# Order of the first loads, of the sines and of the input norms in the opening stage of a GLA / Hyena diffusion step

## The chip, the cores and the metric

One core of a Trainium2 chip runs the kernel. The metric is device microseconds, the median of several executions; lower is better. The core has TensorE (PE, with its weight loads PEld), VectorE (DVE), ScalarE (ACT), GpSimd (POOL) and SyncE (SP); the last three also issue DMAs, each from its own queue.

## The reference, cut to what matters

The whole model step has two layers (one with GLA and retention heads, one with Hyena convolutions and an RG-LRU). The change touches what comes ahead of the first layer's projections:

```python
mod = silu(cond) @ w_mod[layer] + b_mod[layer]              # (1024) @ (1024, 3072), two layers
shift, scale, gate = split(mod, 3)
h = rms_norm(x, norm_g[layer]) * (1 + scale) + shift        # x: 1024 + 128 tokens of 1024

def hyena_filters(L, ...):                                  # L = 1024 and 128
    g = sin(freq1 * (feats @ w1 + b1))
    g = sin(freq2 * (g @ w2 + b2))
    filt = (g @ w3 + b3).reshape(L, 4, 1024)
    return filt * exp(-t * deltas)[:, None, :]
# the Fourier transform of filt is what the long convolutions of layer 2 read
```

## The kernel before

The program is written with a tile framework whose scheduler sets the order on each engine when the kernel is built; each engine then works through its own list strictly in that order and waits on semaphores. `issue_after(x)` and `high_priority(n)` move work in that order.

**The opening stage** (`phase0`) does four things and then `phase1` begins with its projections (`pp` on TensorE).

- The filter network (`filter_mlp`): `ft` times `w1`, a range reduction on VectorE (`fold`, tiles `sv` and `sk`), a sine on ScalarE (tile `g1`), times `w2`, again `fold` and sine (`g2`), for 1152 positions in four pieces of 288. The result goes as a high and a low part into `GA` and `GB`.
- Eight filters (`filters`, n = 0 to 7). Of each, 40 tap products (`mm<-wa,GA` and `mm<-wb,GB`, 256 columns) are multiplied on VectorE by the window `win`, an exponential made on ScalarE (tile `fa`). VectorE's butterflies make an even half (`fd`) and an odd half (in `fa`) from it. TensorE then takes nine leaf groups of four products each (`mm<-fd,fw` and `mm<-fa,fw`): the five even ones, the tap products of filter n+1, the four odd ones. ScalarE copies each group out (`fH`), SyncE stores it to `h_dram`.
- The modulation (`modulation`): for each of two layers, 64 products of the conditioning (`cond`, 32 columns) with 384 columns of `w_mod` into four column groups of PSUM tile `mod`. The 64 loads of `w_mod` (384 KB each, two products) go through GpSimd's queue, from the start on. Two products are issued at a time, as one step of a generator that the leaf groups advance. Layer 0 is done in two parts: three quarters (24 loads) with the first filter, the rest at the end.
- The inputs: x has nine tiles of 128 tokens. A first pass (`start`, beside filter 1) loads all nine on ScalarE's queue into two buffers and takes their sums of squares; `rstd` then gives all nine scales at once. A second pass (`h_tiles`, three tiles after each of filters 1, 2 and 7) loads x again (`x0`), scales it on ScalarE, transposes it on TensorE (`tr<-ident,x`, eight per tile), applies the modulation on ScalarE (`htmp`), and splits it into `hh` (ScalarE) and `hl` (VectorE), which the projections read.

ScalarE uses two activation tables: one with the natural logarithm and the exponential, one with the sine. In the order before, six of the first 18 windows stand ahead of the first sine, and 12 behind the last.

Of the kernel before, what the change touches and what calls it, by code (L numbers as in the profile page):

```python
# [17 lines left out]
P = 128  # L18
# [150 lines left out]
class Step:  # L169
# [61 lines left out]
    def rstd(self, pool, ms, shape, tag, scale=1.0):  # L231

        v = self.t(pool, shape, tag + "v")
        r = self.t(pool, shape, tag + "r")
        q = self.t(pool, shape, tag + "q")
# [10 lines left out]
    def setup(self, po):  # L246
        i, pc = self.i, self.pc
        self.ident = pc.tile([P, P], F32, name="ident")
        self.ld(self.ident, i["k_ident"])
# [4 lines left out]
        self.rows = [po.tile([P, 2, CH], F32, name=f"rows{k}") for k in range(2)]  # L254
# [49 lines left out]
    def modulation(self, layer, p, psm, js=(0, 8), more=None):  # L304
# [3 lines left out]
        row = self.rows[layer]  # L308
        bias = self.t(p, [P, 2, CH], "htmp")
        parts = [(b, max(js[0] - 4 * b, 0), min(js[1] - 4 * b, 4)) for b in range(2)]  # L310
        parts = [x for x in parts if x[1] < x[2]]
        self.nc.gpsimd.memset(bias, 0.0)
        for b, lo, hi in parts:
            for g in range(lo, hi):
                for r in range(2):
                    at = (4 * b + g) * CH
                    self.ld(bias[32 * g + r:32 * g + r + 1, b], i["b_mod"][layer:layer + 1, at:at + CH])
        n = 2
        todo = [(k, j) for k in range(KT) for j in range(*js, n)]
        ws = []  # L320

        def load():
            k, j = todo[len(ws)]
            w = self.t(more, [P, n * CH], "wm", bufs=4) if more and len(ws) % 7 < 4 else self.t(self.pr, [P, D], "wr")[:, :n * CH]
# [11 lines left out]
        for b, lo, hi in parts:  # L336
            s = slice(32 * lo, 32 * hi)
            self.tt(row[s, b], acc[s, b, :CH], bias[s, b], OP.add)
            if b:
                self.sto(self.row_dram[layer, s], row[s, b])  # L340
        if js[0]:
            return
# [30 lines left out]
    def norm_tile(self, p, x, junk, out, tag="n"):  # L373
# [4 lines left out]
        self.ts(out, x, r, OP.mult)  # L378
# [39 lines left out]
    def mlp_loads(self, pt):  # L418
# [4 lines left out]
        ft = self.t(pt, [33, n], "ft")  # L423
        for q, name in enumerate(("hy_b1", "hy_freq1", "hy_b2", "hy_freq2")):
# [9 lines left out]
    def filter_mlp(self, p, pt, ps, loads):  # L434
# [6 lines left out]
        hv, w1, ft, w2 = loads  # L441
        GA = self.t(p, [P, 2 * n + P], "GA", F32R)
# [16 lines left out]
        for c in range(2):  # L459
# [5 lines left out]
            self.ts(v, pm[:, :m], hc[:, 1:2], OP.mult, hc[:, 0:1], OP.add)  # L465
            self.fold(pt, v, g1[:, s], "sk")
        for e in range(2):
            h = slice(64 * e, 64 * e + 64)
            for c in range(2):
# [3 lines left out]
                self.ts(v, pm[:, :m], hc[:, 3:4], OP.mult, hc[:, 2:3], OP.add)  # L473
# [15 lines left out]
        self.nc.gpsimd.dma_start(GB[64:], i["k_ones"])  # L489
# [70 lines left out]
    def windows(self, pt, g):  # L560
# [7 lines left out]
        self.window(0, 18 if g else 6)  # L568
# [34 lines left out]
    def filters(self, p, pi, pt, G, ps, w, others, first, rest):  # L603
# [19 lines left out]
        def leaves(n, g, o, ks, E, L, prompt):  # L623
            for k in ks:
                if n != 1:
                    with self.tc.issue_after(self.last_mm.ins):
                        for z in range(1 if n else 2):
                            next(rest if n else first, None)
                pm = self.t(ps, [P, 512], "mm")
                if k < 8:  # L630
                    self.leaf(pm[:, :C], pm[:, C:], (L, E), k)
                else:
                    for e in range(2):
# [4 lines left out]
                evac = self.nc.scalar.copy(H[:, :, :2].rearrange("p b r c -> p r b c"),  # L638
                                           pm.rearrange("p (r b c) -> p r b c", r=2, b=2))
# [5 lines left out]
            return evac  # L645
# [1055 lines left out]
```

## Time and profile before

| What | us |
|---|---|
| median of 3 executions | 2502.75 (2501.25 to 2506.71) |
| profiled execution, device time | 2499.16 |
| its span | 2497.2 |
| opening stage, to the first `pp` product | 308 |
| TensorE busy in the span | 2414.1 (97%) |

The profile gives the busy time of each engine, the granted clock of TensorE, the DMA traffic, the chain of work that ended last, and for each instruction what ended the idle time ahead of it (in square brackets). TensorE's records overlap, so starts rather than lengths give the pace. A 32-bit product of the leaves or of the modulation leaves two records.

### The profile page before, as it was taken

The page shows a single profiled execution, that of the slowest core. Times are in us where ns is not written, and L with a number is a line of the kernel's source. Part 1 is how long each engine was busy: PE and PEld are TensorE (multiplying, and loading weights), DVE is VectorE, ACT ScalarE, POOL GpSimd, SP SyncE. Part 2 cuts the span into 40 slices and gives each one's busy share as a digit, 9 for nine tenths or more (in the row PEclk, how much of TensorE's full clock was granted, in tenths as well). Part 3 has the DMA queues.
Part 4 walks back from the last instruction along what each step waited for, and adds up shares of the span by engine and source line. Part 5 has one row for each costly group of instructions (what it writes and reads, how often), then busy time and mean ns, then how long its engine had stood idle before and what let it go on. Part 6 is the DMA issues. An engine that isn't in the chain of part 4 may idle for free.

```text
span 2497.2 us, 38502 instructions
## 1 busy us (share of the span) xinstructions
PE 2414.1 (97%) x14681; PEld 2201.0 (88%) x14681; DVE 1660.5 (66%) x3970; ACT 1071.1 (43%) x2355; POOL 72.7 (3%) x149
## 2 busy tenths in 40 slices
PE   5799799999999999999999999999999999999998
PEld 2666699999999999997888999999999999998786
DVE  6588657686664464564234688878887897888632
ACT  4555556564543343353224332223222328888311
POOL 2011000000000000000000000000000000000000
PEclk9899899999999999999999999999999999999999
DMA  7677511121211212225334421222122212114431
GB/s 226 199 233 208 183 47 46 54 60 31 56 52 51 61 46 54 60 83 179 106 115 149 146 65 60 63 72 69 57 62 75 65 43 62 62 62 142 154 98 41
DMA packets 201080, 230.68 MB, mean 92 GB/s; under 512 B 13823, under 2 KB 171743, under 8 KB 200448
## 3 DMA queue, kind: packets, MB, share of 16 engines
q1 hardware_dynamic: 188120, 175.01, 23.1%
q0 software_dynamic: 11104, 48.27, 6.0%
q10 hardware_dynamic: 1672, 4.95, 0.7%
q8 instruction: 115, 1.88, 0.3%
q14 instruction: 69, 0.57, 0.1%
HBM read 172.27 MB, written 55.91 MB: 91 GB/s over the span
## 4 chain that ended last, share of the span: by engine, by line
PE 85%; DVE 6%; ACT 4%; DMA 3%; issue 2%; SPq 0%; POOL 0%; DVEq 0%; ACTq 0%; POOLq 0%
PE pp L211 45%; PE po L211 14%; PE mm L211 5%; PE X L211 5%; PE pd L211 5%; PE o L211 3%; PE tr L215 2%; PE kv L211 2%; PE pg L211 2%; PE mod L211 1%; PE sc L211 1%; PE kv L215 1%; DVE fa L200 1%; DMA wr<-h_dram 1%; DVE cs L200 1%
## 5 line engine op out<-in xcount | busy, mean ns | idle before, releaser
L211 PE MATMUL pp<-gh,wl 128*128 128x384 f32 x1152 | 392.6, 341 | 0.0
L211 PE MATMUL pp<-gh,wh 128*128 128x384 f32 x1152 | 391.6, 340 | 0.7 <-ACT raw L1293 0.6
L211 PE MATMUL pp<-gl,wh 128*128 128x384 f32 x1152 | 391.1, 340 | 0.4 <-DVE gl L200 0.4
L211 PE MATMUL pp<-wh,hh 128*128 128x256 f32 x1152 | 332.7, 289 | 0.0
L211 PE MATMUL pp<-wh,hl 128*128 128x256 f32 x1152 | 328.7, 285 | 0.0
L211 PE MATMUL pp<-wl,hh 128*128 128x256 f32 x1152 | 326.2, 283 | 0.0
L211 PE MATMUL po<-woh,yth 128*128 128x512 f32 x558 | 221.1, 400 | 3.3 <-ACT woh L394 2.8
L211 PEld LDWEIGHTS pp<-wh,hl 128*128 128x128 f32 x1152 | 221.8, 193 | 0.0
L211 PEld LDWEIGHTS pp<-wl,hh 128*128 128x128 f32 x1152 | 220.6, 192 | 0.0
L211 PEld LDWEIGHTS pp<-wh,hh 128*128 128x128 f32 x1152 | 220.2, 191 | 0.0
L211 PEld LDWEIGHTS pp<-gh,wh 128*128 128x128 f32 x1152 | 217.3, 189 | 2.1 <-ACT raw L1293 1.0
L211 PE MATMUL po<-woh,ytl 128*128 128x512 f32 x558 | 218.1, 392 | 1.0 <-DVE ytl L200 1.0
L211 PE MATMUL po<-wol,yth 128*128 128x512 f32 x558 | 219.0, 393 | 0.0
L211 PEld LDWEIGHTS pp<-gh,wl 128*128 128x128 f32 x1152 | 217.2, 189 | 0.9
L211 PEld LDWEIGHTS pp<-gl,wh 128*128 128x128 f32 x1152 | 216.8, 188 | 1.3 <-DVE gl L200 0.7
L200 DVE TENSOR_TENSOR wl<-wr,wh 128x1024 fp32r<-128x1024 f32 (+1 forms) x97 | 118.3, 1220 | 125.7 <-ACT wh L394 125.1
L394 ACT CAST wh<-wr 128x1024 fp32r<-128x1024 f32 (+1 forms) x97 | 101.3, 1045 | 141.2 <-PE pp L211 141.2
L211 PE MATMUL pp<-hh,wh 128*128 128x384 f32 (+1 forms) x408 | 137.6, 337 | 2.1 <-ACT htmp L197 2.1
L211 PE MATMUL pp<-hl,wh 128*128 128x384 f32 (+1 forms) x408 | 137.4, 337 | 0.0
L211 PE MATMUL pp<-hh,wl 128*128 128x384 f32 (+1 forms) x408 | 137.3, 336 | 0.0
L211 PE MATMUL pd<-iv,Y 128*128 128x256 f32 (+1 forms) x576 | 132.0, 370 | 0.0
L211 PEld LDWEIGHTS po<-woh,yth 128*128 128x128 f32 x558 | 104.6, 188 | 26.7 <-ACT woh L394 4.3
(325 smaller groups left out, 4887.3 us busy)
## 6 DMA issues: line engine op xcount, KB each, us to landing
wr<-in_ab_w_in_dram SPq DMA_DIRECT2D x48, 512.0 KB
wr<-in_cd_w_in_dram SPq DMA_DIRECT2D x48, 512.0 KB
H<-h_dram SPq DMA_DIRECT2D x32, 640.0 KB
wr<-in_w_mod_dram POOLq DMA_DIRECT2D x49, 384.0 KB, 4.7
h_dram<-fH SPq DMA_DIRECT2D x112, 128.0 KB
y_dram<-y SPq DMA_DIRECT2D x72, 128.0 KB
y<-y_dram SPq DMA_DIRECT2D x36, 256.0 KB
x<-in_x_sample_dram SPq DMA_DIRECT2D x16, 512.0 KB
```

The source lines that it names most:

```text
L200: return self.nc.vector.tensor_tensor(out=out, in0=a, in1=b, op=op)
L211: self.last_mm = self.nc.tensor.matmul(out, l, r, start=start, stop=stop)
L215: return self.nc.tensor.transpose(out, in_, self.ident)
L394: self.nc.scalar.copy(hi, x)
```

## The change

The change is in the opening stage alone.

- SyncE issues `ident` first. GpSimd copies one column of `ft` (`late`) as soon as that has landed, and only behind this stand its `k_ones` load and the loads of `w_mod`.
- The scaling ahead of each `fold` goes from VectorE to ScalarE (Identity). All 18 first windows stand behind the last sine.
- The pass `start` is gone. Each x tile is loaded once, squared, scaled in place and transposed, in two work items (`norm`, `move`); each leaf group takes the next item. So `rstd` runs nine times on one column instead of once on nine.
- The modulation issues four products at a time, on all four column groups. Layer 0 is done whole (32 loads) with the first filter, with ten load buffers instead of seven; layer 1 follows at one set of four per three leaf groups, with four buffers. Layer 1's bias is loaded after its last product.
- The third set of x tiles is queued at filter 6 instead of after filter 7. The pool of the projections' weight buffers (`pr`) is opened after the stage, where the pool of the modulation's weights (`p0w`) had been.

```diff
     def setup(self, po):
-        self.ident = pc.tile([P, P], F32, name="ident")
-        self.ld(self.ident, i["k_ident"])
...
-    def modulation(self, layer, p, psm, js=(0, 8), more=None):
+    def modulation(self, layer, p, psm, pw, more=None):
...
+        if more:
+            load_bias(more, "bias")
         n = 2
-        todo = [(k, j) for k in range(KT) for j in range(*js, n)]
+        todo = [(k, j) for j0 in (0, 4) for k in range(KT) for j in range(j0, j0 + 4, n)]
...
-        ahead = 7 if more else 3
+        ahead = 10 if more else 4
         for at, (k, j) in enumerate(todo):
-            while len(ws) < min(at + ahead, len(todo)):
+            while len(ws) < min(at + ahead - at % 2, len(todo)):
                 load()
-            for e in range(n):
-                b, g = divmod(j + e, 4)
-                self.mm(acc[32 * g:32 * g + 32, b, :CH], self.cond[:, k], ws[at][:, CH * e:CH * (e + 1)], k == 0, k == KT - 1)
+            if at % 2:
+                if not more:
+                    yield
+                for g in range(4):
+                    self.mm(acc[32 * g:32 * g + 32, j // 4, :CH], self.cond[:, k],
+                            ws[at - 1 + g // n][:, CH * (g % n):CH * (g % n + 1)], k == 0, k == KT - 1)
             yield
...
+        if not more:
+            load_bias(p, "htmp")
...
     def norm_tile(self, p, x, junk, out, tag="n"):
         self.act(junk, x, AF.Square, accum_out=ss)
         r = self.rstd(p, ss, [P, 1], tag, 1.0 / D)
-        self.ts(out, x, r, OP.mult)
+        if out is None:
+            self.act(x, x, AF.Copy, scale=r)
+        else:
+            self.ts(out, x, r, OP.mult)
...
     def filter_mlp(self, p, pt, ps, loads):
+        gate = self.nc.gpsimd.tensor_copy(self.t(pt, [33, 1], "late"), ft[:, n - 1:n])
+        with self.tc.issue_after(gate.ins):
+            self.late = self.nc.gpsimd.memset(self.t(pt, [1, 1], "late2"), 0.0)
...
-            self.ts(v, pm[:, :m], hc[:, 1:2], OP.mult, hc[:, 0:1], OP.add)
+            self.act(v, pm[:, :m], AF.Identity, scale=hc[:, 1:2], bias=hc[:, 0:1])
...
     def windows(self, pt, g):
-        self.window(0, 18 if g else 6)
+        if g:
+            self.window(0, 18)
...
     def filters(self, p, pi, pt, G, ps, w, others, first, rest, work):
+                if work:
+                    work.pop(0)()
                 pm = self.t(ps, [P, 512], "mm")
...
     def phase0(self):
-                first = self.modulation(0, po, psm, (0, 6), pa)
-                for z in range(12):
-                    next(first)
+                with self.tc.issue_after(self.late.ins):
+                    first = self.modulation(0, po, psm, pw, pa)
+                    for z in range(16):
+                        next(first)
-            self.window(6, 18)
-
-            def start():
-                for t in range(NT):
-                    x = self.t(pa, [P, D], "xs", bufs=2)
-                    self.nc.scalar.dma_start(x, self.x_src(t))
-                    self.act(x, x, AF.Square, accum_out=ss[:, t:t + 1])
-                self.rx = self.rstd(self.pc, ss, [P, NT], "xn", 1.0 / D)
+            self.window(0, 18)
...
+                    def norm(t=t, q=q):
+                        if not q:
+                            load(t)
+                        if q < 2:
+                            load(t + 1)
+                        tmp = self.t(po, [P, KT, P], "htmp")
+                        self.norm_tile(po, xs[t], tmp.rearrange("p k c -> p (k c)"), None, "xn")
+                        tmps[t] = tmp
+
+                    def move(hi=hi, lo=lo, t=t):
+                        self.mod_transpose(pst, 0, t, xs[t], tmps[t])
+                        self.split(hi, lo, tmps[t])
...
             self.filters(p, pi, pt, G, ps, w, {
-                0: start, 1: lambda: (s2.close(), h_tiles(0)), 2: lambda: h_tiles(1),
-                7: last}, first, rest())
+                0: lambda: (s2.close(), h_tiles(0)), 1: lambda: h_tiles(1), 6: last},
+                first, self.modulation(1, po, psm, pw), work)
```

The scheduler's order at three places, before and after. First ScalarE ahead of the first sine; `cl` is the SiLU of the conditioning, `g_18` and `g_20` are `g1`, and `wa` is a filter weight. Before:

```order
L197 ACTIVATE cl_111<-cl_111 128x16
L197 ACTIVATE cl_112<-cl_111 128x16
L197 ACTIVATE win_143<-delta_141,negt 128x256
L197 ACTIVATE cl_111<-cl_111 128x16
L197 ACTIVATE win_143<-delta_141,negt 128x256 x5
L597 CAST wa_160<-raw_8_152 128x512
L197 ACT_TABLE_LOAD
L197 ACTIVATE g_18_178<-sv_183 128x288
```

The same place now:

```order
L197 ACTIVATE cl_108<-cl_108 128x16
L197 ACTIVATE cl_109<-cl_108 128x16
L197 ACTIVATE sv_178<-tr_175,hc_169 128x288
L197 ACTIVATE cl_108<-cl_108 128x16
L197 ACTIVATE sv_190<-tr_187,hc_169 128x288
L611 CAST wa_151<-raw_8_143 128x512
L197 ACT_TABLE_LOAD
L197 ACTIVATE g_20_173<-sv_178 128x288
```

The six windows, and their wait for `delta`, have left the place; two scalings stand there.

Second TensorE between the tap products of two filters in the middle of the stage. Before:

```order
L211 MATMUL mod_1041<-wr_1332,cond 32x384 x2
L211 MATMUL mm_1375<-fd_1358,fw_167 128x256 x4
L211 MATMUL mod_1041<-wr_1345,cond 32x384 x2
L211 MATMUL mm_1391<-fa_1170,fw_167 128x256 x4
L211 MATMUL mod_1041<-wr_1371,cond 32x384 x2
L211 MATMUL mm_1407<-fd_1358,fw_167 128x256 x4
L211 MATMUL mod_1041<-wr_1387,cond 32x384 x2
```

And now:

```order
L211 MATMUL mod_1077<-wr_1403,cond 32x384 x2
L211 MATMUL mod_1077<-wr_1405,cond 32x384 x2
L211 MATMUL mm_1585<-fa_1263,fw_158 128x256 x4
L211 MATMUL mm_1598<-fa_1263,fw_158 128x256 x4
L211 MATMUL mm_1607<-fa_1263,fw_158 128x256 x4
L211 MATMUL mod_1077<-wr_1444,cond 32x384 x2
L211 MATMUL mod_1077<-wr_1446,cond 32x384 x2
```

Two modulation products stood ahead of every leaf group; now four stand ahead of every third.

Third TensorE at the end of the stage. Before:

```order
L211 MATMUL mm_2483<-fa_2226,fw_167 128x256 x4
L215 MATMUL tr_2415<-ident,x_454_2411 128x128 x4
L215 MATMUL tr_2424<-ident,x_454_2411 128x128 x4
L211 MATMUL mm_2492<-fa_2226,fw_167 128x256 x4
L211 MATMUL mm_2501<-fa_2226,fw_167 128x256 x4
L211 MATMUL mm_2510<-fa_2226,fw_167 128x256 x4
L215 MATMUL tr_2439<-ident,x_458_2435 128x128 x4
L215 MATMUL tr_2448<-ident,x_458_2435 128x128 x4
L215 MATMUL tr_2463<-ident,x_462_2459 128x128 x4
L215 MATMUL tr_2472<-ident,x_462_2459 128x128 x4
L211 MATMUL pp_2566<-hh_918,wh_2559 96x384
```

And now:

```order
L211 MATMUL mm_2534<-fa_2197,fw_158 128x256 x4
L211 MATMUL mm_2543<-fa_2197,fw_158 128x256 x4
L211 MATMUL mm_2552<-fa_2197,fw_158 128x256 x4
L211 MATMUL mm_2561<-fa_2197,fw_158 128x256
L215 MATMUL tr_2417<-ident,x_440_2324 128x128 x4
L215 MATMUL tr_2426<-ident,x_440_2324 128x128 x4
L211 MATMUL mm_2561<-fa_2197,fw_158 128x256 x3
L211 MATMUL pp_2621<-hh_740,wh_2614 96x384
```

The last two tiles stood bare behind the last leaf group; now one tile stands in it and the others ahead of it. Layer 1's modulation transposes have gone from the middle of the stage to a place behind 91 of the `pp` products.

## Rows read from the trace of the kernel before

**Rows 1.** Page: one kind of modulation load; size, median us from issue to landing.
```profile
wr<-in_w_mod_dram POOLq DMA_DIRECT2D x49, 384.0 KB, 4.7
```

**Rows 2.** Busy time by stretch; the first row names the columns.
```profile
core 0: us, PE busy (x) PEld busy (x) DVE busy (x) ACT busy (x) POOL busy (x), PEclk, DMA share, GB/s
0.00:54.00 54.00, 23.89 (x117) 11.07 (x117) 33.15 (x73) 24.63 (x61) 14.45 (x32) 0.96 0.76 243
54.00:128.60 74.60, 58.79 (x287) 45.26 (x287) 49.14 (x86) 40.98 (x87) 4.46 (x10) 0.85 0.59 189
128.60:226.00 97.40, 97.24 (x491) 63.49 (x491) 80.58 (x131) 51.35 (x110) 18.70 (x38) 1.00 0.77 227
226.00:308.00 82.00, 68.91 (x365) 53.56 (x364) 56.44 (x91) 44.56 (x93) 6.86 (x16) 0.94 0.63 195
308.00:2497.20 2189.20, 2165.23 (x13425) 2027.65 (x13425) 1441.16 (x3592) 909.57 (x2007) 28.26 (x54) 1.00 0.25 76
```

**Rows 3.** DMA queues from 7 to 11 us: packets, MB, share of 16 engines.
```profile
q0 software_dynamic: 320, 1.57, 100.2%
q1 hardware_dynamic: 18, 0.00, 0.6%
```

**Rows 4.** Timeline from 0 to 22 us, ScalarE and VectorE: start, length, engine, work, idle before.
```profile
15.73 0.51 ACT L197 ACTIVATE win<-delta,negt 128x256 f32<-128x256 f32 x1 [5.32 <-DMA delta<-in_k_delta_dram]
...
17.10 0.57 DVE L205 TENSOR_SCALAR sv<-tr,hc 128x288 f32<-128x288 f32 x1
...
20.16 0.44 ACT L197 ACTIVATE g<-sv 128x288 f32<-128x288 f32 x1
```

**Rows 5.** Timeline from the last sine to the first leaf group.
```profile
37.50 0.44 ACT L197 ACTIVATE g<-sv 128x288 f32<-128x288 f32 x1 [2.56 <-DVE sv L205]
...
40.97 4.90 ACT L197 ACTIVATE win<-delta,negt 128x256 f32<-128x256 f32 x12
...
53.94 3.75 PE L211 MATMUL mm<-fd,fw 128*128 128x256 f32 x8 [8.73 <-DVE fd L200]
```

**Rows 6.** Timeline of TensorE in filter 1.
```profile
99.61 3.78 PE L211 MATMUL mm<-fd,fw 128*128 128x256 f32 x8 [6.10 <-ACT fH L642]
```

**Rows 7.** Waits to 310 us: who waited for whom; total, times, longest.
```profile
ACT xs L197 <- DMA xs<-in_x_sample_dram: 11.3, 7, 2.8
```

**Rows 8.** Chain of work: a leaf group, two modulation products, tap products with a group.
```profile
170.07 1.92 PE mm L211 x8
171.99 0.77 PE mod L211 x4
172.76 6.78 PE mm L211 x48
...
201.86 6.79 PE mm L211 x48
```

**Rows 9.** Timeline of TensorE: one modulation product, eight transposes, bare leaf groups.
```profile
156.68 0.83 PE L211 MATMUL mod<-wr,cond 128*32 128x384 f32 x2
157.44 1.09 PE L215 MATMUL tr<-ident,x 128*128 128x128 f32 x8
...
269.99 7.07 PE L211 MATMUL mm<-fa,fw 128*128 128x256 f32 x32
279.05 1.97 PE L211 MATMUL mm<-fd,fw 128*128 128x256 f32 x8 [1.99 <-DVE fd L200]
```

**Rows 10.** Busy time by stretch: VectorE's whole work on filter 7.
```profile
266.00:288.40 22.40, 20.41 (x109) 18.13 (x109) 22.28 (x35) 6.31 (x14) 0.60 (x2) 1.00 0.51 162
```

**Rows 11.** Timeline of VectorE: a small step of the norm, a tile's low half.
```profile
103.86 0.17 DVE L200 TENSOR_TENSOR xnq<-xnr 128x9 f32<-128x9 f32 x1 [0.82 <-ACT xnr L197]
...
124.28 1.23 DVE L200 TENSOR_TENSOR hl<-htmp,hh 128x1024 fp32r<-128x1024 f32 x1 [0.61 <-ACT hh L394]
```

**Rows 12.** Timeline of TensorE at the end of the stage.
```profile
303.94 1.97 PE L215 MATMUL tr<-ident,x 128*128 128x128 f32 x8 [6.09 <-ACT x L197]
...
308.05 0.63 PE L211 MATMUL pp<-hh,wh 128*96 128x384 f32 x1 [2.14 <-ACT htmp L197]
```

More of the change, by code (lines that the diff above doesn't have):

```diff
@@ L231, in rstd @@
     def rstd(self, pool, ms, shape, tag, scale=1.0):
-        v = self.t(pool, shape, tag + "v")
-        r = self.t(pool, shape, tag + "r")
-        q = self.t(pool, shape, tag + "q")
+        w = self.t(pool, [shape[0], 3, shape[1]], tag + "w")
+        v, r, q = (w[:, k] for k in range(3))
         self.ts(v, ms, scale, OP.mult, EPS, OP.add)
@@ L301, in silu_sig, with load_bias @@
         self.act(a, a, AF.Exp)
-    def modulation(self, layer, p, psm, js=(0, 8), more=None):
+    def modulation(self, layer, p, psm, pw, more=None):
         i = self.i
         acc = self.t(psm, [P, 2, 512], "mod")
[L308 to L317, printed above, removed]
+        row = self.t(p, [P, 2, CH], "rows")
+        bias = [None]
+        def load_bias(src, tag):
+            b_ = bias[0] = self.t(src, [P, 2, CH], tag)
+            self.nc.gpsimd.memset(b_, 0.0)
+            for b in range(2):
+                for g in range(4):
+                    for r in range(2):
+                        at = (4 * b + g) * CH
+                        self.ld(b_[32 * g + r:32 * g + r + 1, b], i["b_mod"][layer:layer + 1, at:at + CH])
+        if more:
+            load_bias(more, "bias")
         n = 2
-        todo = [(k, j) for k in range(KT) for j in range(*js, n)]
+        todo = [(k, j) for j0 in (0, 4) for k in range(KT) for j in range(j0, j0 + 4, n)]
         ws = []
@@ L472, in filter_mlp @@
                 v = self.t(pt, [P, m], "sv", bufs=2)
-                self.ts(v, pm[:, :m], hc[:, 3:4], OP.mult, hc[:, 2:3], OP.add)
+                self.act(v, pm[:, :m], AF.Identity, scale=hc[:, 3:4], bias=hc[:, 2:3])
                 lo, hi = (2 * e + c) * m, (2 * e + c + 1) * m
@@ L601, in filter_weights, with filters @@
         return wa, wb
-    def filters(self, p, pi, pt, G, ps, w, others, first, rest):
+    def filters(self, p, pi, pt, G, ps, w, others, first, rest, work):
         C = 256
@@ L667, in filters @@
                 pass
+            if n < 6 and n in others:
+                others[n]()
+        for x in work:
+            x()
+        for z in rest:
+            pass
     def h_store(self, o, g, slot, src):
@@ L724, in h_tiles, with load @@
                     t = 3 * c + q
-                    x = self.t(po, [P, D], "x0")
-                    self.ld(x, self.x_src(t))
-                    self.act(x, x, AF.Copy, scale=self.rx[:, t:t + 1])
-                    tmp = self.t(po, [P, KT, P], "htmp")
-                    self.mod_transpose(pst, 0, t, x, tmp)
-                    s = slice(q * P, (q + 1) * P)
-                    self.split(self.hT[0][c][:, :, s], self.hT[1][c][:, :, s], tmp)
-            def rest():
-                yield from self.modulation(1, po, psm)
-                yield from self.modulation(0, po, psm, (6, 8))
+                    s = slice(q * P, (q + 1) * P)
+                    hi, lo = (x[c][:, :, s] for x in self.hT)
+                    def load(t):
+                        xs[t] = self.t(po, [P, D], "x0", bufs=2)
+                        self.ld(xs[t], self.x_src(t))
+                    def norm(t=t, q=q):
[9 more added lines that the diff above has]
+                        self.split(hi, lo, tmps[t])
+                    work.extend((norm, move))
             def last():
```

38 lines of the change are left out of this document (19 added, 19 removed).

## The prediction

> **What bounds the kernel now.** I read the table by stretch first, since the page's 97% for TensorE is a mean over stages [rows 2]. From 308 us on TensorE works 2165.23 of 2189.20 us, and the change touches nothing there. Ahead of that it stands 30.1 of 54.0 us, 15.8 of 74.6, 0.2 of 97.4 and 13.1 of 82.0, in all 59.2, and the granted clock is 0.85 in the second stretch and 0.94 in the fourth. So there are four stages with different limits. The reader should see which wait ends last in each.
>
> To 54 us it is the filter network. ScalarE waits 5.32 us for `delta` before its first window, although nothing that the network needs hangs on a window [rows 4]; the SiLU of the conditioning stands behind that window in ScalarE's list, and VectorE's first range reduction behind the SiLU's product. The first sine starts at 20.16, the last at 37.50; twelve windows end at 45.87, the first leaf group starts at 53.94 after 8.73 us of idle time [rows 4, 5]. From 54 to 128.60 it is ScalarE's list: the pass over x holds it for 11.3 us of DMA waits [rows 7], the copies out of PSUM stand behind these, and TensorE stops for 6.10 us at one of them [rows 6]. From 128.60 to 226 TensorE itself is the bound, 97.24 of 97.40 us [rows 2]. At the end TensorE waits 6.09 and 2.14 us for the last two tiles [rows 12].
>
> **The change part by part.** *Start of the network.* ScalarE gets back the 5.32 us and six windows of 4.90/12 = 0.41 us, 2.4 in all, and takes over two scalings ahead of the first sine, about 0.45 each (a sine of the same size takes 0.44) [rows 4, 5]: 6.8 us less, of which I take 6. It could be 2, if the filter weight whose cast still stands ahead of the table load lands no earlier than now, and 9 if the first loads also land sooner. VectorE loses six scalings of 0.57 in its chain, 3.4 us [rows 4]. The six windows come back behind the last sine, 2.4 us. Sum 6 + 3.4 - 2.4 = 7: the first leaf group at 47 instead of 53.94.
>
> What lets the loads land sooner: between 7 and 11 us GpSimd's queue moved 320 packets and SyncE's 18, with `delta` and the first weights issued and waiting [rows 3]. The change holds GpSimd's loads back until `ft` has landed, some 3 us. The Trainium skill, "DMA: Bandwidth & Descriptors", section "Queues, rings and completion order", says that an engine takes turns between its queues packet by packet; by that the small loads would never have been starved, and holding the big ones back would give nothing. These rows speak against it here; what it would make of the time is the third rival below.
>
> *Filters 0 and 1, from 47 us to the first even group of filter 2 (now 128.60).* A leaf group costs 7.07/4 = 1.77 [rows 9], the 40 tap products 6.78 - 1.92 = 4.86 [rows 8]. Two modulation products cost 0.77 themselves, and a group beside them 1.92 instead of 1.77, so 0.92 [rows 8]. A single one takes from 156.68 to 157.44, 0.76 [rows 9]: two on different column groups run at once. That four do too, no row shows; the bounds are 0.92 and twice that, and I take 0.92, since the second product cost nothing. TensorE's list: 18 groups 31.9, two sets of taps 9.7, eight sets of four 7.4, three tiles of transposes at 1.09 [rows 9] 3.3; sum 52.3. Add 3 for VectorE's butterflies: behind four bare groups TensorE waits 1.99 us for the next filter's even half [rows 9], and there are two such places, with a tile's work beside them. Add 4 (0 to 10) for `w_mod`: layer 0 now needs 32 loads instead of 24 ahead of the last odd groups, 3.1 MB more, 13 us at the 243 GB/s of the first stretch [rows 2] but 8 at the 392 that 1.57 MB in 4 us make [rows 3], and the ten buffers can fill while the network runs. So 47 + 59 = 106, 22 us earlier than now (11 to 32).
>
> *Filters 2 to 7, from there to the first projection (now 308, that is 179.4 us).* TensorE: 54 groups 95.6, five sets of taps 24.3, sixteen sets of four 14.7, seven tiles 7.6; sum 142.2. Now the same stretch holds 40 pairs, 36.8. But VectorE comes close: a filter costs it 22.28 [rows 10], a tile 1.23 for `hl` and now five steps of 0.17 for its own norm [rows 11], so up to 24.4 a filter; five of these and a last filter of 20 on TensorE make 142. Two engines with the same load that wait for each other in turn don't reach either sum. The ceiling is today's period between two sets of taps, 201.86 - 172.76 = 29.1 [rows 8], where VectorE is slack: 5 x 29.1 + 20 = 165.5. I take 152, nearer the floor, because in the 97.4 us stretch such handovers cost TensorE 0.2 us. Gain 27 (14 to 37). The last filter's 20 are nine groups 15.9, two sets 1.8 and two tiles 2.2. The end is in this sum: the waits of 6.09 and 2.14 [rows 12] go, since the last tile's transposes stand inside the last leaf group and 48 `pp` products on other tiles cover its split.
>
> *Bias and late modulation.* Layer 1's bias loads now wait for the last tile's split, and VectorE's `rows` addition for them, with the projections' next weight splits queued behind it. It costs 0 to 5, I take 2: 91 products stand ahead of the transposes that need it.
>
> *At no cost.* One load of x instead of two takes 4.7 MB and nine issues from ScalarE's queue. Three slices in one `rstd` tile are the same instructions. Nine squares and nine scalings stay. Eighteen small ScalarE steps for logarithm and exponential lie beside a ScalarE that works 51.35 of 97.40 us [rows 2], but in its strict order, so they are in the second rival. The four bias loads more lie on a queue with nothing urgent behind them. Weights for the projections come into buffers that are free once the last `w_mod` load is used, seven groups from the end.
>
> Sum: 22 + 27 - 2 = 47. From the profiled execution's 2499.16 that is 2452. The median of the runs is 3.6 above it, so 2502.75 - 47 = 2456.
>
> **The rivals.** *More comes out:* the network gains 9, no load is late and VectorE hides, so 142 for the last stretch: 32 + 37 = 69, 2434 at the far end; around 2440 as a case. For it: TensorE's wait of 0.2 in 97 us. Against it: VectorE has the same load there.
>
> *The norms become the bound.* Logarithm and exponential wait in ScalarE's list behind copies and weight casts, and VectorE, strict in order too, stands in front of its butterflies for them. VectorE had one such wait, 0.82 us, for all nine tiles [rows 11]; now nine. If they and the butterflies keep the period at 29.1, the gain in the last stretch is 14 instead of 27: 47 - 13 = 34, 2469.
>
> *Load order gives nothing:* queues share the engines anyway, the first weights land as now, and the network gains 0 to 2 instead of 7: 47 - 6 = 41, 2462.
>
> *It doesn't do what it says:* four products run two and two. Sixteen sets cost 0.77 more in a stretch where TensorE is one of two bounds, 12 us: 47 - 12 = 35, 2468.
>
> *Slower:* x holds ScalarE. The square of a tile waits in ScalarE's list for a load that could be issued only when one of two buffers came free; copies out of PSUM stand behind it and TensorE behind these, as at 99.61 [rows 6]. A load of 384 KB lands in 4.7 us [rows 1], so one of 512 KB in about 6.3. If every tile held ScalarE for all of that, nine would cost 56 us against the 47: 2512. It decides from 5.2 us a tile. Against it: the load is issued one tile ahead, and in the old pass seven such waits made 11.3 us together [rows 7].
>
> **How the numbers follow.** Forecast (2444 to 2467) 0.47; more comes out 0.14; norms 0.18; load order 0.09; two and two 0.07; slower 0.05. The range must hold 8 in 10: from 2436, near the best sum, to 2483, where the low ends of all terms add up (network 2, filters 0 and 1 at 11 in all, 14 behind them, 5 lost at the end). What is left out is the slower rival and the tails. About 0.2% is what a measurement can tell from no change, 5 us. Faster by more than that 0.93, within it 0.02, slower 0.05.
>
> **What would show it.** The first sine near 14 us and the first leaf group near 47; the first even group of filter 2 near 106; the first projection near 262; a modulation set with eight records in 0.8 us; VectorE at 90% between. The forecast is wrong if ScalarE shows waits for x or for VectorE's norm steps ahead of copies out of PSUM, if TensorE waits for `w_mod` ahead of leaf groups, or if the stretch behind the first projection isn't as long as before.

## The result, and the profile of the changed kernel

The changed kernel takes 2463.18 us, median of four runs (2460.74 to 2466.54), against 2503.59 for the kernel before (2501.25 to 2506.71). The ratio is 0.9839, 95% interval 0.982 to 0.9858. The forecast was 2456 and its range 2436 to 2483: right in direction and within the range, 7 us too fast. The profiled execution took 2460.76 us with a span of 2459.0.

The same view as [rows 2], busy time by stretch, with the new borders (first leaf group, first even group of filter 2, of filter 4, first projection). After the length of a stretch come the busy times of TensorE, its weight loads, VectorE, ScalarE and GpSimd, then TensorE's granted clock, the share of the DMA engines and GB/s.

```profile
core 0: us, PE busy (x) PEld busy (x) DVE busy (x) ACT busy (x) POOL busy (x), PEclk, DMA share, GB/s
0.00:53.49 53.49, 27.76 (x133) 11.84 (x133) 30.77 (x67) 28.29 (x68) 18.27 (x41) 0.98 0.88 300
53.49:111.01 57.52, 53.06 (x302) 40.92 (x303) 50.84 (x96) 36.76 (x81) 5.57 (x12) 0.96 0.59 195
111.01:171.89 60.88, 51.86 (x305) 41.15 (x305) 53.66 (x96) 48.98 (x107) 7.73 (x16) 1.00 0.67 206
171.89:266.86 94.97, 90.04 (x512) 72.53 (x513) 82.81 (x146) 51.98 (x114) 11.11 (x24) 1.00 0.66 212
266.86:2459.00 2192.14, 2164.57 (x13431) 2027.59 (x13431) 1441.66 (x3601) 909.60 (x2008) 29.38 (x57) 1.00 0.25 76
```

Set against the borders of before [rows 2], the two profiled spans differ by 38.2 us:

| stretch | before | after | gain | forecast |
|---|---|---|---|---|
| to the first leaf group | 53.94 | 53.49 | 0.45 | 7 |
| filters 0 and 1 | 74.66 | 57.52 | 17.1 | 15 |
| filters 2 to 7 | 179.45 | 155.85 | 23.6 | 27 |
| behind the first projection | 2189.15 | 2192.14 | -3.0 | -2 |

The border of 128.60 in before is a pair of modulation products; filter 2's first leaf group follows at 129.60. From leaf group to leaf group the two middle gains are 18.1 and 22.6.

So the sum held because three of its four terms were near. The first failed altogether. Inside the third the even groups of filters 2 to 7 start at 111.0, 141.5, 171.9, 196.1, 220.5 and 245.3: two periods (the time from one filter's first even group to the next one's) of 30.4, then 24.2 to 24.8. Before, the periods of filters 2 to 6 were 32.3, 29.1, 29.1, 33.4 and 25.6. Filter 2 and filter 4 of after, as in the first table:

```profile
111.01:141.45 30.44, 25.98 (x153) 20.57 (x153) 27.10 (x52) 25.42 (x57) 3.87 (x8) 1.00 0.64 194
171.89:196.10 24.21, 24.21 (x145) 19.73 (x145) 23.60 (x42) 14.24 (x32) 3.87 (x8) 1.00 0.60 196
```

Timeline of ScalarE at the start, and of TensorE where filters 0, 2, 3 and 4 and the projections begin (start, length, engine, work, in brackets the idle time ahead and who ended it):

```profile
16.79 0.62 ACT L611 CAST wa<-raw 128x512 fp32r<-128x512 f32 x1 [8.06 <-DMA raw<-in_hy_w_dram]
17.42 1.28 ACT L197 ACT_TABLE_LOAD   x1
18.71 0.78 ACT L197 ACTIVATE g<-sv 128x288 f32<-128x288 f32 x2
20.69 0.62 ACT L612 CAST wi<-raw 128x512 fp32r<-128x512 f32 x1 [1.20 <-DMA raw<-in_hy_skip_dram]
```

```profile
53.49 3.75 PE L211 MATMUL mm<-fd,fw 128*128 128x256 f32 x8 [6.48 <-DVE fd L200]
111.01 1.97 PE L211 MATMUL mm<-fd,fw 128*128 128x256 f32 x8 [2.67 <-DVE xnw L200]
141.45 1.97 PE L211 MATMUL mm<-fd,fw 128*128 128x256 f32 x8 [1.99 <-DVE xnw L200]
171.89 1.97 PE L211 MATMUL mm<-fd,fw 128*128 128x256 f32 x8 [1.98 <-DVE fd L200]
266.86 0.39 PE L211 MATMUL pp<-hh,wh 128*96 128x384 f32 x1 [1.85 <-issue]
```

ScalarE stood 8.06 us for filter 0's weights, and the sine's table and the first sine queued behind their cast. The answer to [rows 7], waits from 54 to 267 us (who waited for whom; total, times, longest):

```profile
ACT fH L654 <- DMA h_dram<-fH: 14.3, 10, 3.4
ACT wa L611 <- DMA raw<-in_hy_w_dram: 6.6, 1, 6.6
PE mm L211 <- DVE fd L200: 8.5, 2, 6.5
PE mm L211 <- DVE xnw L200: 5.8, 3, 2.7
ACT x L197 <- DVE xnw L200: 5.3, 3, 2.7
DVE xnw L200 <- ACT xnw L197: 4.1, 3, 2.3
```

The old pass over x and its 11.3 us are gone. The waits of copies out of PSUM for the stores of earlier ones (there are three buffers `fH`) have grown; before, they were 5.3 us from 54 to 309. New are waits of ScalarE, VectorE and TensorE for each other around `xnw`, a tile's norm. The 6.6 us are for filter 1's weights, at 50 to 57 us. Last, a leaf group and a set of four modulation products in the chain of waits, as in [rows 8] (start, length, work):

```profile
63.00 0.78 PE mod L211 x8
63.79 1.92 PE mm L211 x8
```

Eight records are four products, and 0.78 is what two cost before, 0.77. Four run at once. The trace of before has this too, in filter 0, where layer 0's pairs are issued two by two:

```profile
62.13 0.85 PE L211 MATMUL mod<-wm,cond 128*32 128x384 f32 x8
62.91 1.99 PE L211 MATMUL mm<-fd,fw 128*128 128x256 f32 x8
67.54 0.84 PE L211 MATMUL mod<-wr,cond 128*32 128x384 f32 x4
68.21 0.81 PE L211 MATMUL mod<-wm,cond 128*32 128x384 f32 x4
```

By the kernel's order the four products at 62.13 lie on four column groups, and take 0.78 to the next start. The two pairs at 67.54 lie on the same two groups, and the next start is at 68.96, 1.42 later.

### The profile page after: what moved, and what is told of

It reads as the page before. It is cut to its first block, busy times and chain, and to the rows that moved or that the text cites. A ratio compares the mean times of both kernels' runs of the same rounds, so it can differ in the third digit from the quotient of the medians.

```text
span 2459.0 us, 38543 instructions
## 1 busy us (share of the span) xinstructions
PE 2387.3 (97%) x14681; PEld 2194.0 (89%) x14681; DVE 1659.7 (67%) x4003; ACT 1075.6 (44%) x2377; POOL 72.1 (3%) x150
## 4 chain that ended last, share of the span: by engine, by line
PE 81%; DVE 8%; ACT 5%; DMA 4%; issue 1%; SPq 0%; DVEq 0%; ACTq 0%; POOL 0%
PE pp L211 44%; PE po L211 13%; PE X L211 5%; PE pd L211 5%; PE mm L211 3%; PE o L211 3%; PE tr L215 2%; PE kv L211 2%; PE pg L211 2%; DMA h_dram<-fH 1%; PE sc L211 1%; DVE fa L200 1%; PE kv L215 1%; DVE cs L200 1%; DVE cs L936 1%
## 5 line engine op out<-in xcount | busy, mean ns | idle before, releaser
L211 PE MATMUL po<-woh,yth 128*128 128x512 f32 x558 | 220.5, 399 | 3.0 <-ACT woh L401 2.8
```

The source lines that it names most:

```text
L211: self.last_mm = self.nc.tensor.matmul(out, l, r, start=start, stop=stop)
```

## The experiments

Each kernel is an edit of the changed kernel, or of another edit where it says so, compared by medians (the changed kernel's is 2463.18) and by where a stage begins. The ratios are all to the kernel before. Stage times are from one traced execution of each kernel, and executions of one kernel lie 3 to 7 us apart, once 12; a shift of one or two us in a trace, and a difference of medians whose intervals overlap, is not told from chance.

### What held the start: four kernels

**Big loads behind filter 0's weights.** The gate on `w_mod` waits for `raw` instead of `ft`:

```diff
-        gate = self.nc.gpsimd.tensor_copy(self.t(pt, [33, 1], "late"), ft[:, n - 1:n])
+        late = self.t(pt, [P, 2, 2], "late")
+        self.nc.gpsimd.tensor_copy(late[:, 0], self.raw[0][:, :, 255])
+        gate = self.nc.gpsimd.tensor_copy(late[:, 1], self.raw[1][:, :, 255])
```

> The changed kernel, with the big w_mod loads held back until filter 0's weights have landed instead of ft. In the changed kernel the first sine starts at 18.71 us because the cast of those weights, which land near 16.7, stands ahead of the sine table in ScalarE's list, and 2463.2 is its median. Theory A (the weights land late because w_mod's packets share the engines with them from 5.5 us on): they land near 10 to 11, first sine 13 to 14, first leaf group 5 us earlier than 53.49, and the time falls by 3 to 5 to about 2459, unless the later w_mod loads make TensorE wait ahead of the odd leaf groups of filter 1. Rival B (load order gives nothing, the small loads take their time by themselves): the weights land at 15 to 17 as now, first sine 17 to 19, time 2461 to 2466.

2466.70 (ratio 0.9852, 0.9838 to 0.9865). ScalarE's timeline and TensorE's first even groups of filters 0 and 2:

```profile
9.51 0.62 ACT L614 CAST wa<-raw 128x512 fp32r<-128x512 f32 x1 [0.68 <-DMA raw<-in_hy_w_dram]
10.15 1.28 ACT L197 ACT_TABLE_LOAD   x1
11.44 0.85 ACT L197 ACTIVATE g<-sv 128x288 f32<-128x288 f32 x2
```

```profile
49.26 3.58 PE L211 MATMUL mm<-fd,fw 128*128 128x256 f32 x8 [3.70 <-DVE fd L200]
114.80 1.97 PE L211 MATMUL mm<-fd,fw 128*128 128x256 f32 x8 [2.67 <-DVE xnw L200]
```

Theory A was right on the loads: the weights are there 7 us sooner, the first sine starts at 11.44 instead of 18.71, the first leaf group 4.2 us earlier. It was wrong on the time, which did not fall. None of the gain reached the end: filter 0 takes 38.3 us from there instead of 30.4, and filter 2 begins 3.8 us later.

**Casts behind the sines.** The two casts of filter 0's weights move behind the last sine, loads untouched:

```diff
+            w = self.filter_casts(pt, w)
             self.window(0, 18)
```

> The changed kernel, with filter 0's two weight casts put behind the last sine in ScalarE's list, load order untouched. Theory A (the cast alone holds the first sine): table load right behind the second scaling, first sine near 13, last sine near 29, first leaf group near 48, 5 us earlier, time about 2458. Rival C (the chain to the first leaf group is set elsewhere: delta and the skip row, which land near 20.5, or VectorE's range reductions): first sine earlier, but first leaf group within 2 us of 53.49 and time 2461 to 2464.

2461.31 (ratio 0.9841, 0.9822 to 0.986): not to be told from the changed kernel. The first sine starts at 9.99, but the first leaf group at 53.98. VectorE and TensorE between them, from 29 us:

```profile
29.48 0.29 DVE L289 COPY cols<-tr 128x128 f32<-128x128 f32 x1 [8.16 <-PE tr L215]
```

```profile
29.00 0.45 PE L215 MATMUL tr<-ident,sg 128*128 128x128 f32 x1 [8.55 <-DMA sg<-in_ab_head_g_dram]
```

Rival C in its numbers, though the cause is none of those that it named. VectorE stands 8.16 us in the middle of the last range reduction, for a copy to `cols`, whose transpose waits for one of the eleven small vectors. ScalarE's last sine then starts at 31.98 instead of 34.29. With one stall gone the next is late.

**Both edits.**

> Both edits together: big loads behind filter 0's weights, and their casts behind the sines. Theory A: no more than the better of the two alone, first leaf group near 47 to 48, time about 2458, since each removes the same wait. Rival C: first leaf group stays above 51.5 and the time within 2 us of 2463.

2462.37 (0.9837, 0.9824 to 0.9851). First leaf group 50.36, filter 0's period 34.5 instead of 30.4, first even group of filter 2 at 112.10 instead of 111.01. Both expectations missed something: the leaf group moved by 3 us, more than rival C allowed, and the time did not move, against theory A.

**The small vectors too.** On top of both edits, `vectors` is worked behind filter 0's taps:

```diff
         a = taps(w)
+        others["vec"]()
```

> The kernel with both edits on the start, in which the small vectors (sg to cols: eleven small loads, two transposes, two copies on VectorE) are worked behind filter 0's taps instead of ahead of the last sines. In it the second copy to cols at 30.07 held VectorE 3.94 us, and wb and the taps behind it. Theory V (each stall at the start uncovers the next, and this was the last but one): taps from 29 instead of 32.8, first leaf group 46 to 47.5; then, if transfers bind behind it (theory T), filter 0's period grows by as much and the time stays at 2460 to 2464; if not, 2457 to 2459.

2467.03 (0.9846, 0.9832 to 0.9859), above the expected 2464. The first leaf group comes at 48.55, filter 0's period is 37.4, and filter 2 begins at 113.10. Three of these four kernels brought the first leaf group forward, by 3 to 5 us, and in each trace filter 0 lost as much or more.

### Why filter 0 takes it back: transfers

The kernel with both edits, with half of layer 0's `w_mod` loads left out (the products of odd k read the tile of the k before):

```diff
+            if more and k % 2:
+                ws.append(ws[-2])
+                return
```

> The kernel with both edits on the start (w_mod behind filter 0's weights, casts behind the sines; 2462.4 us, first leaf group 50.4, filter 0's period 34.5), in which half of layer 0's w_mod loads, 6.3 MB, are left out: the products of odd k read the tile of the k before. Theory T (the start is bound by what all transfers move: 350 to 380 GB/s from 20 to 50 us, so what the small loads win w_mod and filter 1's weights lose): first leaf group no later than 50.4, filter 0's period back to 28 to 30.5, so the first even group of filter 2 at 104 to 107 instead of 112.1 and the time 2455 to 2458. Rival E (engines bind): filter 0's period stays above 33 and the time within 2 us of 2462.

2459.10 (0.9819, 0.9806 to 0.9833). First leaf group 49.83, filter 0's period 31.1, first even group of filter 2 at 107.79 instead of 112.10. Busy time by 10 us (columns as in the first table), first with all loads, then with half:

```profile
20.00:30.00 10.00, 4.84 (x22) 1.42 (x24) 4.04 (x11) 7.36 (x20) 3.58 (x7) 1.00 1.04 365
30.00:40.00 10.00, 9.48 (x61) 4.99 (x61) 5.81 (x12) 7.11 (x17) 3.55 (x8) 1.00 1.02 377
40.00:50.00 10.00, 4.20 (x38) 1.84 (x37) 9.13 (x8) 1.44 (x3) 3.23 (x6) 0.94 1.03 370
60.00:70.00 10.00, 7.94 (x51) 5.64 (x50) 2.84 (x9) 3.93 (x7) 0.88 (x2) 0.96 0.96 365
```

```profile
40.00:50.00 10.00, 1.89 (x16) 1.08 (x16) 9.97 (x10) 2.90 (x5) 0.00 (x0) 0.78 0.56 170
60.00:70.00 10.00, 10.00 (x73) 8.06 (x73) 4.41 (x11) 4.45 (x8) 0.00 (x0) 1.00 0.37 125
```

With all loads the DMA engines are full from 10 to 50 us and again from 60 to 70. ScalarE waits 10.0 us for filter weights between 44 and 90, with halved loads 2.7:

```profile
ACT wa L620 <- DMA raw<-in_hy_w_dram: 10.0, 2, 5.7
```

```profile
ACT wa L623 <- DMA raw<-in_hy_w_dram: 2.7, 1, 2.7
```

Filter 0's loss shrinks with the bytes, as theory T has it. Each number is a little short of it (31.1 against 28 to 30.5, 107.8 against 104 to 107, 2459.1 against 2455 to 2458), so a part of filter 0's loss has another cause, and the medians' intervals overlap (0.9824 to 0.9851 with all loads). In the kernel with all loads the start moves a fixed amount of data at 365 to 377 GB/s; what one load gains by going first another loses, and the next filter's weights were the ones that lost. The first leaf group itself came only 0.5 us earlier with half of the loads, so their bytes are not what holds it at 50.

### The load order undone alone

The gate is taken out; `w_mod` loads start as soon as GpSimd comes to them.

```diff
-                with self.tc.issue_after(self.late.ins):
-                    first = self.modulation(0, po, psm, pw, pa)
+                first = self.modulation(0, po, psm, pw, pa)
```

> The changed kernel without the gate: the big w_mod loads start as soon as GpSimd comes to them, all else as in the changed kernel. It is the load order undone by itself. Theory A (the small loads lose their place to w_mod): ident, hv and filter 0's weights land 2 to 4 us later, first sine 20 to 23, time 2465 to 2467. Rival B (load order gives nothing): first sine within 1 us of 18.71 and time within 2 us of 2463.

2465.67 (0.9851, 0.9838 to 0.9865): 2.5 us more, with intervals that overlap. The trace does show it: first sine 21.44 instead of 18.71, first leaf group 55.70 instead of 53.49, first projection 272.0 instead of 266.9. The cast that waits for filter 0's weights starts at 19.51 instead of 16.79, 2.7 us later, and with the later gate it came 7.3 earlier. So holding the big loads back does move the small ones.

The rule that the prediction quoted from the Trainium skill, "DMA: Bandwidth & Descriptors", section "Queues, rings and completion order", is that an engine takes turns between its queues, packet by packet. The trace of before agrees with it in part: from 11 to 14 us SyncE's queue moved 205 packets and GpSimd's 197, about one for one, but 0.07 MB against 0.98. Small packets got few bytes out of their turns there. So turns alone don't keep small loads from being late, as the prediction took them to. From 8 to 11 us SyncE's queue moved none, although `negt` was issued at 7.47; why not stays open. For the time the rival of load order gave the better number, 2462, but not for its reason: order does move the loads, and what it gave was lost again in filter 0.

### Four products at a time, undone

```diff
-            if at % 2:
-                if not more:
-                    yield
-                for g in range(4):
+            if at % 2 and not more:
+                yield
+            for e in range(n):
+                g = j % 4 + e
```

> The changed kernel with the modulation's products issued two at a time again, all else as it is. A set of four took 0.78 us, as a pair did before, so each set now costs 0.77 more on TensorE. If TensorE binds behind filter 1: sixteen sets of layer 1, 12 us, and up to eight of layer 0, 6 us: 2475 to 2481. If TensorE's idle time in the 30.4 us periods takes it up, only the sets in the 24.4 us periods cost (8 sets, 6 us) : 2467 to 2471. If four at a time was worth nothing: 2461 to 2465.

2476.26 (0.9887, 0.9873 to 0.9901): 13.1 us more. Layer 0's two pairs of a set still stand back to back, and the first even group of filter 2 comes at 111.4, as before the edit. So the price lies with layer 1's sixteen sets. It is 13.1/16 = 0.82 each on average, near what a set of four costs itself (0.78), but it doesn't fall evenly. Filter 2, with three sets, takes 30.6 instead of 30.4; filter 3, with three too, 38.1 instead of 30.4; filters 4 to 6 are 1.8 to 2.7 longer and filter 7 is 2.9 shorter. So idle time took the price up in filter 2 and not in filter 3; why filter 3 lost three times its share wasn't tried.

### One pass for the norms, undone

All squares are formed in one pass at filter 0's odd half, one `rstd` serves nine tiles, and each tile is loaded a second time (for room, `wb` has one buffer):

```diff
+            def start():
+                for t in range(NT):
+                    x = self.t(po, [P, D], "x0", bufs=2)
+                    self.nc.scalar.dma_start(x, self.x_src(t))
+                    self.act(x, x, AF.Square, accum_out=ss[:, t:t + 1])
+                self.rx = self.rstd(self.pc, ss, [P, NT], "xn", 1.0 / D)
...
-                        self.norm_tile(po, xs[t], tmp.rearrange("p k c -> p (k c)"), None, "xn")
+                        self.act(xs[t], xs[t], AF.Copy, scale=self.rx[:, t:t + 1])
```

> The changed kernel with the norms as before: one pass over all nine tiles for the squares at filter 0's odd half, one rstd for all, then each tile loaded again and scaled. Theory N1 (the single pass is what gave filters 0 and 1 their gain): ScalarE waits some 11 us for x again, the first even group of filter 2 comes 8 to 12 us later than 111.0, and the periods of filters 2 and 3 fall by 1 to 2 from 30.4 since no norm waits stand in them: time 2466 to 2472. Rival N2 (the norms' hand-overs between ScalarE and VectorE cost as much as the pass did): periods fall to 26 to 27, time 2459 to 2465.

2486.22 (0.9923, 0.9909 to 0.9937): 23.0 us more, where theory N1 expected 3 to 9. TensorE's timeline in filter 1, whose period grew from 27.2 to 58.6:

```profile
97.54 3.44 PE L211 MATMUL mm<-fd,fw 128*128 128x256 f32 x8 [3.99 <-ACT fH L658]
104.19 0.58 PE L211 MATMUL mm<-wa,GA 128*128 128x256 f32 x1 [2.97 <-ACT fH L654]
111.44 1.97 PE L215 MATMUL tr<-ident,x 128*128 128x128 f32 x8 [2.96 <-ACT x L197]
123.38 0.58 PE L211 MATMUL mm<-wb,GB 128*128 128x256 f32 x1 [5.63 <-ACT wb L614]
```

The pass holds ScalarE's list for 11.8 us of loads (11.3 in [rows 7]); the copies, the transposes' inputs and the weight casts stand behind it, and TensorE stops at each of them. How much of the 5.63 us for `wb` comes from its single buffer was not separated, so not all of the 23.0 is shown to be the pass's. What rival N2 saw is there too, only small: filters 2 and 3 take 25.7 and 28.4 instead of 30.4 each.

### The long periods: three kernels

**A fourth buffer for the copies.** Room comes from one buffer instead of two for the weight casts, which also moves the cast of the filter after next back in ScalarE's list:

```diff
-                H = self.t(p, [P, 2, 3, P], "fH", bufs=3)
+                H = self.t(p, [P, 2, 3, P], "fH", bufs=4)
...
-        wa = self.t(pt, [P, 2, C], "wa", F32R, bufs=2)
-        wb = self.t(pt, [P, 2, C], "wb", F32R, bufs=2)
+        wa = self.t(pt, [P, 2, C], "wa", F32R)
+        wb = self.t(pt, [P, 2, C], "wb", F32R)
```

> The changed kernel with four buffers fH for the copies out of PSUM instead of three (room from the weight casts wa and wb, one buffer each instead of two). In the changed kernel the even halves of filters 2 to 7 start at 111.0, 141.5, 171.9, 196.1, 220.5 and 245.3 us: two periods of 30.4, where x tiles are worked, then 24.2 to 24.8. Theory S (the stores bind): ScalarE's copies wait 14.3 us for the stores of h_dram to 275 us; the fourth buffer takes most of it, the two long periods fall to 26 to 28, time 2452 to 2457 against 2463. Rival N (VectorE and ScalarE bind through the norm and split of a tile): the wait moves to another place, periods stay within 1 us, time 2461 to 2466.

2455.22 (0.9805, 0.9792 to 0.9819): 8 us less. The waits from 54 to 261 us:

```profile
ACT x L197 <- DVE xnw L200: 6.0, 4, 2.7
PE mm L211 <- DVE xnw L200: 5.7, 3, 2.7
ACT fH L654 <- DMA h_dram<-fH: 2.1, 3, 1.2
```

The wait for stores fell from 14.3 to 2.1 us. The periods of filters 2 and 3 fell to 28.6 and 29.6 only, filter 7's from 21.6 to 19.8, and the first projection starts at 260.4 instead of 266.9. So theory S gave the time within its range, but not for its reason alone: the waits around `xnw` are as long as they were, and the first leaf group, ahead of all copies, came 1.4 us earlier. How the 6.5 us divide between buffers and the moved casts was not separated.

**The norm on ScalarE alone**, on top of that; VectorE's five small steps, the refinement of the reciprocal root among them, are left out:

```diff
+            self.act(r, ss, AF.Ln, scale=1.0 / D, bias=self.eps)
+            self.act(r, r, AF.Exp, scale=-0.5)
```

> The kernel with four fH buffers (2455.2 us, periods of filters 2 and 3 at 28.6 and 29.6, of 4 to 6 at 24.1 to 24.8), in which a tile's norm for x stays on ScalarE alone: logarithm with 1/1024 and epsilon as its scale and bias, exponential, scaling; VectorE's five small steps, and with them the refinement of the reciprocal root, are left out. Theory H (the hand-overs between ScalarE and VectorE, each strict in order, make the long periods): both periods fall by 2 to 3 us, filter 1 by 1 to 2, time 2448 to 2451. Rival F (a tile's own work, about 5 us of ScalarE and 2 of VectorE, makes them): periods within 1 us, time 2453 to 2456.

2451.97 (0.9794, 0.978 to 0.9807). Filters 1 to 3 take 29.2, 29.0 and 24.8 instead of 26.9, 28.6 and 29.6: filter 3 became 4.8 us shorter, filter 1 2.3 longer, and the first projection is 2.4 us earlier. The time lies between theory H's range and rival F's, and the interval overlaps that of four buffers alone, so no gain in time is shown. The pattern is neither's: without the hand-overs filter 3 got shorter and filters 1 and 2 did not.

**Work on x at every third leaf group:**

```diff
-                if work:
+                at = 0 if n >= 6 else (0, 8, 2, 4, 6, 1, 3, 5, 7).index(k) % 3
+                if work and not at:
```

> The changed kernel with the work on x (norm, then transposes and split) taken up at every third leaf group instead of at every one, so that tiles 0 to 5 lie over four filters and not two and a half. Theory D (two tiles in one filter are too dense: queues in order block each other): the two periods of 30.4 become four of at most 26, time 2452 to 2458. Theory F (a tile costs about 3 us of period wherever it lies, since VectorE, ScalarE and TensorE are near full): periods near 28, the same sum, time 2461 to 2465.

2457.57 (0.9811, 0.9796 to 0.9825). Filters 1 to 4 take 26.6, 26.2, 31.0 and 28.2, together 112.0; in the changed kernel they take 27.2, 30.4, 30.4 and 24.2, together 112.2. The first projection moved by 1.0 us. The time is in theory D's range, but the pattern is theory F's: the same sum. Of the 5.6 us the two traces have 3.2, 2.2 of them behind the first projection, where nothing was edited; the intervals of the two kernels just overlap.

**Both, four buffers and spread work:**

> Four fH buffers and the work on x at every third leaf group together. Alone, the first ended filter 7 at 260.4 us instead of 266.9 (2455.2 us), the second left the sum of filters 1 to 4 at 112 us, as in the changed kernel, and ended at 265.9 (2457.6). Theory D2 (with the stores' wait out of the way, a tile costs less where its neighbours are bare leaf groups): filters 1 to 4 in 104 to 107 us, first projection at 255 to 258, time 2450 to 2453. Theory F2 (a tile costs what it costs, wherever it lies): filters 1 to 4 within 2 us of the 109.3 of four buffers alone, first projection at 259 to 261, time 2453 to 2457.

2451.74 (0.9796, 0.9783 to 0.9809), the fastest kernel that computes all that the reference does: 11.4 us less than the changed one. Filters 1 to 4 take 26.0, 24.5, 30.4 and 25.0, together 105.9, first projection 258.2. So in the traces spreading the tiles pays once the copies don't wait for stores, as theory D2 has it: 105.9 against 109.3 with four buffers alone. In the medians that is 3.5 us, with intervals that overlap. What is left is filter 3. Waits of TensorE from 133.7 to 164.1 us:

```profile
PE mm L211 <- ACT fH L655: 1.7, 2, 1.0
PE mm L211 <- ACT wb L614: 1.5, 1, 1.5
```

From 132.71 to 150.0 ScalarE works there with hardly a gap: twelve of the eighteen windows for the next group of channels, a tile and the copies, in one list. That this is what keeps filter 3 at 30.4 is read from the trace and wasn't tried. The two waits are 3.2 us; TensorE is also busy 27.3 us there, against 24.6 in filter 2, at a granted clock of 0.94 instead of 1.00.

## Why the prediction was right, and where it wasn't

- **Start of the network: wrong, 0.45 us instead of 7.** In the prediction's own terms: to the first sine 1.45 us were gained (20.16 to 18.71) and not 6, from first to last sine 1.76 (17.34 to 15.58) and not 3.4, and behind the last sine 2.76 were lost (16.44 to 19.20) where it had 2.4. The step that failed first took 6 us for ScalarE's freed time, with 2 as the low end if filter 0's weights landed no earlier. It came out below that low end: the weights landed late because `ft` frees the big loads at 5.5 us, too soon for them, and the first sine starts at 18.71, not 14. The step had a second fault: it took a gain of the first leaf group for a gain of the whole, and its 4 us for late loads stayed the same however early that group came. The experiments took the cast, the big loads and the small vectors out of that chain, brought the first leaf group to 48.55, and gained nothing. The DMA engines were full and filter 0's period grew by what was won; halving the loads undid most of that, not all. Counted in bytes, the stage moved 16.0 MB (300 GB/s over 53.49 us) against 13.1 (243 over 54.0 [rows 2]), some 3 MB more. That is the size of the eight added `w_mod` loads, whose cost the prediction had charged to filters 0 and 1. What holds the first leaf group at 48 to 50 when those stalls are gone stays open.
- **Filters 0 and 1: right, 57.5 us against 59.** Four products run at once, which no row had shown, though the trace of before held such rows (62.13). TensorE works 53.1 of the 57.5, near the 52.3 of its list; the list has three tiles here and seven behind, where x has nine, and two came here. The list is at full speed, and there TensorE gained too: its granted clock in the stretch went from 0.85 to 0.96, and its busy time from 58.79 to 53.06 with more records, 302 for 287 [rows 2]. The 4 us for late `w_mod` loads did not come as waits of products for loads.
- **Filters 2 to 7: right in size, 155.9 against 152, wrong in shape.** The prediction took one old period, 29.1, for a ceiling, where before had 32.3 and 33.4 as well. Two periods were 30.4, and the next three 24.2 to 24.8, against 22.3 of VectorE's work [rows 10] and 23.2 of TensorE's (15.9 for leaf groups, 4.9 for taps, 2.4 for products). It had also counted one tile a filter, 24.4 us of VectorE; the kernel works two tiles in each of filters 2 and 3, and VectorE is busy 27.1 and 26.6 there. Beside that, these two hold the norm rival's waits and one that the prediction had not named, that of copies for stores, 14.3 us from 54 to 267; with a fourth buffer it fell to 2.1.
- **Behind the first projection: 3 us lost against 2, and not by the cause given.** The first product of the next form comes 41.19 us earlier in after (308.01 against 349.20), just as the first projection does: the late bias and modulation cost nothing there. The loss lies between 900 and 1100 us further on, where TensorE idles 5.8 us instead of 2.7. That stretch was edited in no kernel here, and the whole part behind the first projection takes from 2188.7 to 2195.6 us over the kernels of this study, so 3 us are not told from chance. That the number is near the forecast of 2 is luck. What moves it stays open.
- **Rivals.** Load order gives nothing: right on the time of the start, wrong on the loads, which a gate does move. More comes out fell with the first term. Two and two fell (0.78 for four; undone, +13.1 us). Norms: true of filters 2 and 3 alone. Slower fell: ScalarE waits for x 2.6 us, once.
- **Parts, each undone alone:** norms 23.0 (with one buffer `wb` less), four products 13.1, load order 2.5 (not told from nothing), together 38.6 of the 40.4 us. That they add up is not shown. The order of the sines, the scaling on ScalarE, layer 0 as a whole ahead and the last tiles at filter 6 weren't undone by themselves.

## What to carry to other kernels

Where a start runs on loads, first add up the bytes that must land before its end: if the DMA engines are full, as here, another order mostly chooses who waits. In a list that is worked strictly in order, a pass that waits for loads can cost more than its waits (11.8 us of them cost up to 23), because everything behind it is late for somebody else. Two engines that are each busy for 85 to 90% of a period and wait for each other in small steps need more than the longer of their sums; a buffer more for the copies between them, with the casts that moved for its room, gave 8 us here. And look in the trace of before for a row of what the change will do: the one for four products at once was there.

## What the runs showed of the hardware

- Four products on four groups of 32 columns of TensorE took 0.78 us, two 0.77 [rows 8]; two pairs on the same two groups took 1.42.
- A leaf group behind a long wait ran at half speed: its four products (eight records) took 3.75 us after 6.48 us of idle time at 53.49, and 1.97 after 2.67 at 111.01. From 50 to 60 us the granted clock is 0.66, so part of that stretch ran at 1.2 and not 2.4 GHz:

```profile
50.00:60.00 10.00, 6.51 (x24) 4.16 (x24) 10.00 (x18) 1.85 (x5) 1.31 (x3) 0.66 0.55 184
```

- Holding GpSimd's big loads back until SyncE's small ones had landed brought the cast that waits for these from 16.79 to 9.51 us; from 11 to 14 us of before the two queues moved 205 and 197 packets, 0.07 and 0.98 MB. With half of layer 0's `w_mod` loads gone the engines' share from 40 to 50 us fell from 1.03 to 0.56.
